# A hybrid attention and state-space layer on one core: the state-space products as tiles of the TensorE array, the result transposes in the input's PSUM bank, one table load per pair, table copies on GpSimd

## The chip, the cores and the metric

The kernel runs on one core of one Trainium2 chip. The metric is device time in microseconds (us) of one execution, taken as the median of several runs. The engines of the core are named as the profile names them: PE is TensorE (PEld its weight loads), DVE is VectorE, ACT is ScalarE, POOL is GpSimd, SP is SyncE, which here issues most DMAs. A "pass" below is one PE record of the profile: a float32 matmul is recorded as two passes, a float32r or bf16 one as one.

## The reference

One decoder layer over 2048 tokens of width 1024, float32:

```python
h = rmsnorm(x, g_mix) * (1 + sc_m) + sh_m          # sc, sh, gt: six vectors, silu(c) @ w_ada + b_ada
q, k, v, f_logit, u = split(h @ w_in)              # 512, 512, 512, 8, 512 columns
attn = rmsnorm(forgetting_attention(q, k, v, log_sigmoid(f_logit + b)), g_attn_out)   # 8 heads x 64
ssm  = rmsnorm(s5_ssm(u, ...), g_ssm_out)
x = x + gt_m * (concat([attn, ssm]) @ w_out)
h = rmsnorm(x, g_ffn) * (1 + sc_f) + sh_f
gate, val = split(h @ w_up)                        # 2 x 2816 columns
x = x + gt_f * ((silu(causal_dwconv(gate)) * val) @ w_down)
return rmsnorm(x, g_final)

def s5_ssm(u, ...):                                # 32 groups x 16 channels, 64 complex states each
    bu = einsum(u, ((lam_bar - 1) / lam) * b)      # lam_bar = exp(lam * dt)
    h  = scan over time: h[t] = lam_bar * h[t-1] + bu[t]
    z  = gelu(real(einsum(h, c)) + d_skip * u)
    return z * sigmoid(z @ w_glu + b_glu)          # per group, 16 x 16
```

## The kernel before

Large products are written as three float32r products of high and low parts. The tokens are worked in four blocks of 512 (`NB`, `TB`). The order in which instructions stand on each engine is not that of the source: a scheduler sets it when the program is built, from priorities (`tc.high_priority()` around `ssm`), from the buffers that the pools have, and from its own times.

The state-space part has two stages.

**Tables** (`ssm_tables`). The 32 groups are 16 pairs; a pair's two groups of 64 states fill the 128 partitions. Four batches `q` of four pairs each build, on DVE, powers of the eigenvalues times the output and input matrices (`f_re`, `f_im`, `e_re`, `e_im`) and rotations (`c_t_`, `s_t_`), and write them to DRAM: `tab_d[q]`, 1024 columns per pair (256 for the input, 256 cosine, 256 sine, 256 for the output from the state), and `tt_d[q]`, one 128x128 Toeplitz matrix per group (8 steps x 16 channels). The Toeplitz entries come from PE products of `bbr`/`bbi` (64 rows, 16 columns) with `f_re`/`f_im` (lines 797 and 798), one group after the other in one PSUM bank (`prep_ps`; `misc_ps = prep_ps` in this function). DVE copies them out (line 799), adds the skip term (lines 802 and 804), and eight DMAs per half write shifted copies from a zero-padded tile `kz` (line 807). The same bank serves the transposes of `e_re`/`e_im` (line 812).

**Pairs** (`ssm`). Time is cut into 256 chunks of 8 steps. For pair `p`, `stage_a` loads the tables and two tiles `ft` whose off-diagonal halves stay zero (lines 833 to 841), transposes the input (`in_ps`, line 853), makes the chunk sums `ss_ps` with the 64-column halves of the array (line 861), and DVE turns, scans and turns back (lines 866 to 879, result `hs`). `stage_b`, written one pair later, makes `y` of each group as one Toeplitz product and two products from the state (lines 887 to 889, 128 rows each), then GELU and GLU on ACT and DVE (lines 892 to 907, product `g_ps` line 901), transposes the result (`tr_ps`, line 912) and copies it to `vout` (line 915), which goes to `ssm_d` (line 941). PSUM holds one bank each: `in` (in_ps, ss_ps), `y` (y_ps), `out` (g_ps, tr_ps).

What stands around the pairs on PE are the projections of q, k (line 485) and v (line 452), and attention of block 0: lines 967 (row maxima), 1012 to 1015 (scores), 1033 and 1037 (times v). After the last pair, `mix_t(0)` loads the `ssm_d` rows, squares them (line 1211), takes a reciprocal root in small DVE steps (lines 185 to 195), scales the rows (line 1217), transposes them (line 1221), and `out_proj(0)` follows (line 1247). The up and down products of the MLP need its result.

Of the kernel before, what the change touches and what calls it, by code (L numbers as in the profile page):

```python
# [12 lines left out]
F32 = mybir.dt.float32  # L13
# [3 lines left out]
AF = mybir.ActivationFunctionType  # L17
ALU = mybir.AluOpType
# [4 lines left out]
P = 128  # L23
# [102 lines left out]
def hybrid_layer(ctx, tc, x, c_t, w_ada, b_col, gains, w_flat, bf_row, a_re, a_im, log_dt,  # L126
# [535 lines left out]
    def ssm_tables(pp):  # L662
        misc_ps = prep_ps
# [12 lines left out]
        Q.dma_start(ci, sc_im)  # L676
        ds_t = tl("ds", [16, NG])
        Q.dma_start(ds_t, dskip)

# [38 lines left out]
        V.tensor_tensor(out=fi, in0=fi, in1=den, op=ALU.mult)  # L718
        bbr, bbi, t16 = tl("bbr", [P, NPAIR, 16]), tl("bbi", [P, NPAIR, 16]), tl("t16", [P, NPAIR, 16])
        b3 = [P, NPAIR, 16]  # L720
# [34 lines left out]
        def batches(marks):  # L755


            kz = tl("kz", [16, 4, 16, 16])
            G.memset(kz[:, :, 0:8, :], 0.0)
            kt = kz[:, :, 8:16, :]  # L760
            for q in range(4):
                with tc.issue_after(marks[q].ins):
# [28 lines left out]

                    for half in range(2):
                        ps = misc_ps()
                        rs = slice(half * 64, half * 64 + 64)
                        for pr in range(4):
                            po = ps[0:16, pr * P : (pr + 1) * P]
                            T.matmul(po, lhsT=bbr[rs, 4 * q + pr, :], rhs=f_re[rs, pr, 0:8, :], start=True, stop=False)
                            T.matmul(po, lhsT=bbi[rs, 4 * q + pr, :], rhs=f_im[rs, pr, 0:8, :], start=False, stop=True)
                        V.tensor_copy(kt, ps[0:16, :].rearrange("c (g m d) -> c g m d", g=4, m=8))
                        dg = tl("dg", [16, 4, 16])  # L800
                        dsq = ds_t.rearrange("c (q p h) -> c q h p", q=4, h=2)[:, q, half, :]
                        V.tensor_tensor(out=dg, in0=ident[0:16, 0:16].unsqueeze(1).broadcast_to([16, 4, 16]),
                                        in1=dsq.unsqueeze(2).broadcast_to([16, 4, 16]), op=ALU.mult)
                        V.tensor_tensor(out=kt[:, :, 0, :], in0=kt[:, :, 0, :], in1=dg, op=ALU.add)
                        dst = tt_d[q].rearrange("(p h) k n -> h k p n", h=2)[half]
                        for j in range(8):
                            Q.dma_start(dst[j * 16 : (j + 1) * 16], kz[:, :, 8 - j : 16 - j, :].rearrange("c g m d -> c g (m d)"))
                    for pr in range(4):
                        wb = tl("wb", [P, 2 * P])
                        ps = misc_ps()  # L810
                        for a, e in enumerate((e_re, e_im)):
                            T.transpose(ps[:, a * P : (a + 1) * P], e[:, pr].rearrange("p j c -> p (j c)"), ident)
                        A.copy(wb, ps[:, 0 : 2 * P])
                        Q.dma_start(td[:, pr, 0:256], wb)
# [7 lines left out]
    def ssm(sp, sps):  # L822
# [3 lines left out]
        V.tensor_scalar(out=hb, in0=hb, scalar1=0.5, scalar2=None, op0=ALU.mult)  # L826
        fts = [sp.tile([P, 2, 2, P], F32, name=f"ft{i}", bufs=1) for i in range(2)]
        for ft in fts:
            G.memset(ft, 0.0)

        def stage_a(p, vin):
            tab = sp.tile([P, 768], F32, name="tab", tag="tab")
            Q.dma_start(tab, tab_d[p // 4][p % 4, :, 0:768])
            ft = fts[p % 2]
            for g in range(2):
                rs = slice(g * 64, g * 64 + 64)
                Q.dma_start(ft[rs, :, g, :], tab_d[p // 4][p % 4, rs, 768:1024].rearrange("p (a n) -> p a n", a=2))
            ttg = sp.tile([P, 2, P], F32, name="ttg", tag="ttg")
# [43 lines left out]
        def stage_b(p, vout, ft, ttg, glt, ug, hs):  # L882

            yp = sps.tile([P, 512], F32, name="y_ps", tag="y", bufs=1)
            for g in range(2):
                yo = yp[:, g * 256 : (g + 1) * 256]
                T.matmul(yo, lhsT=ttg[:, g, :], rhs=ug[:, g, :], start=True, stop=False)
                T.matmul(yo, lhsT=ft[:, 0, g], rhs=hs[:, 0, 0:256], start=False, stop=False)
                T.matmul(yo, lhsT=ft[:, 1, g], rhs=hs[:, 1, 0:256], start=False, stop=True)

            y2 = sp.tile([P, 512], F32, name="y2", tag="y2", bufs=1)
# [3 lines left out]
            z = sp.tile([P, 512], F32, name="z", tag="z")  # L895
# [3 lines left out]
            th = sp.tile([P, 512], F32, name="th", tag="th")  # L899
            for g in range(2):  # L900
                T.matmul(gp[:, g * 256 : (g + 1) * 256], lhsT=glt[:, g, :], rhs=z[:, g * 256 : (g + 1) * 256],
                         start=True, stop=True)
            for g in range(2):
                A.activation(th[:, g * 256 : (g + 1) * 256], gp[:, g * 256 : (g + 1) * 256], AF.Tanh, scale=0.25,
                             bias=hb[:, 2 * p + g : 2 * p + g + 1])
            o4 = th
            V.scalar_tensor_tensor(out=o4, in0=th, scalar=1.0, in1=z, op0=ALU.add, op1=ALU.mult)
            c0 = (p % 4) * 32
            pt = sps.tile([P, 512], F32, name="tr_ps", tag="out", bufs=1)
            for kb in range(2):  # L910
                for g in range(2):
                    T.transpose(pt[:, (2 * kb + g) * P : (2 * kb + g + 1) * P],
                                o4[:, g * 256 + kb * P : g * 256 + (kb + 1) * P], ident)
            for kb in range(2):
                A.activation(vout[kb][:, :, c0 : c0 + 32].rearrange("k t (g c) -> k g t c", g=2),
                             pt[:, kb * 256 : (kb + 1) * 256].rearrange("k (g t c) -> k g t c", g=2, t=8), AF.Copy, scale=0.25)

# [1024 lines left out]
```

## Time and profile before

| | |
|---|---|
| median of 3 runs | 2587.67 us (2587.0 to 2597.44) |
| the profiled execution | 2591.18 us, span 2589.5 us, mean granted TensorE clock 0.983 |
| busy share | PE 96%, PEld 79%, DVE 79%, ACT 48%, POOL 6% |
| table stage, first to last Toeplitz product | 82.6 to 248.8 us |
| pairs, first chunk sum to last result transpose | 350.8 to 577.5 us |
| first product of `out_proj(0)` | 622.3 us |

Times in the profile are counted from the start of the span. The profiled execution took 3.5 us more than the median. Rows of the timeline give the start, the duration (successive equal instructions merged, with their count) and, in brackets, the idle time before and what ended it; passes overlap, so the distance from start to start is what a pass costs, not its duration. Rows of the windows give the length, then busy time and records of PE, PEld, DVE, ACT and POOL, then the granted clock, the DMA engines' busy share and their GB/s.

### The profile page before, as it was taken

How to read it: one execution, taken by the hardware profiler on the slowest of the kernel's cores; microseconds unless marked ns; L12 is line 12 of the kernel's file. 1: busy time of each engine (PE TensorE's matmuls, PEld its weight loads, DVE VectorE, ACT ScalarE, POOL GpSimd, SP SyncE). 2: the span in 40 equal slices, each digit the busy share in tenths (PEclk: the TensorE clock that was granted, in tenths of full speed). 3: DMA queues.
4: the chain of work that ended last, by engine and by line, in shares of the span. 5: the costliest groups of instructions: out<-in, count | busy, mean ns of one | idle time of the engine just before them, and what ended most of it. 6: DMA issues, size and time to landing. Idle time of an engine off the chain costs nothing.

```text
span 2589.5 us, 35781 instructions
## 1 busy us (share of the span) xinstructions
PE 2494.1 (96%) x12107; PEld 2044.2 (79%) x12107; DVE 2048.6 (79%) x3954; ACT 1253.0 (48%) x2122; POOL 151.7 (6%) x160
## 2 busy tenths in 40 slices
PE   6899999998999999999999999999989999999997
PEld 3788877887788888888878888888768888887876
DVE  7989688976787878877877777776589889886777
ACT  3323255654454545555555655556554555553213
POOL 0001000000000000000000000000002333320000
PEclk8999999999899999999999999999999999999998
DMA  8477987667556655656556555556733443447573
GB/s 313 153 256 223 309 257 210 200 184 244 178 185 219 209 185 184 196 179 211 189 198 226 185 179 186 177 184 219 256 101 130 166 160 134 159 153 286 196 279 119
DMA packets 269608, 516.37 MB, mean 199 GB/s; under 512 B 27985, under 2 KB 114897, under 8 KB 269425
## 3 DMA queue, kind: packets, MB, share of 16 engines
q1 hardware_dynamic: 267600, 508.84, 59.6%
q0 software_dynamic: 1280, 4.20, 0.4%
q8 instruction: 96, 1.57, 0.3%
q10 hardware_dynamic: 544, 1.05, 0.1%
q14 instruction: 88, 0.71, 0.1%
HBM read 374.32 MB, written 139.59 MB: 198 GB/s over the span
## 4 chain that ended last, share of the span: by engine, by line
PE 73%; DMA 10%; DVE 10%; ACT 2%; issue 2%; SPq 2%; POOL 0%; POOLq 0%; ACTq 0%; DVEq 0%
PE ff_ps L1273 18%; PE ff_ps L1247 6%; PE up_x L1397 5%; PE up_z L1397 4%; PE up_y L1397 4%; PE ff_ps L1305 3%; PE ff_ps L1307 3%; PE ff_ps L1306 3%; PE o_ps L1033 2%; PE o_ps L1037 2%; DMA wada<-in_w_ada 2%; PE qs_ps L485 2%; PE acc_x L1627 2%; DMA w_raw<-in_w_flat 2%; PE vq_ps L485 1%
## 5 line engine op out<-in xcount | busy, mean ns | idle before, releaser
L86 ACT CAST w_hi<-w_raw 128x1024 fp32r<-128x1024 f32 (+4 forms) x187 | 173.6, 929 | 273.3 <-DMA w_raw<-in_w_flat 63.4
L1273 PE MATMUL ff_ps<-h_hi,w_hi 128*128 128x512 f32 x704 | 276.7, 394 | 1.0 <-ACT h_hi L403 0.8
L1273 PE MATMUL ff_ps<-h_hi,w_lo 128*128 128x512 f32 x704 | 276.7, 393 | 0.9 <-DMA w_lo<-wlo 0.9
L1273 PE MATMUL ff_ps<-h_lo,w_hi 128*128 128x512 f32 x704 | 276.8, 393 | 0.0
L87 DVE TENSOR_TENSOR w_lo<-w_raw,w_hi 128x1024 fp32r<-128x1024 f32 (+4 forms) x187 | 199.6, 1067 | 54.1 <-ACT w_hi L86 48.9
L1024 DVE TENSOR_TENSOR pl<-pf,ph 128x512 fp32r<-128x512 f32 (+1 forms) x320 | 194.5, 617 | 23.3 <-ACT ph L1023 22.6
L1023 ACT CAST ph<-pf 128x512 fp32r<-128x512 f32 (+1 forms) x320 | 178.0, 568 | 58.6 <-PE o_ps L1033 54.8
L1032 DVE TENSOR_TENSOR acc<-acc,pf 128x512 f32<-128x512 f32 (+2 forms) x264 | 159.2, 604 | 45.1 <-ACT pf L1022 39.5
L1273 PEld LDWEIGHTS ff_ps<-h_hi,w_hi 128*128 128x128 f32 x704 | 132.7, 189 | 29.0 <-ACT h_hi L403 1.5
L1273 PEld LDWEIGHTS ff_ps<-h_hi,w_lo 128*128 128x128 f32 x704 | 132.8, 189 | 28.6 <-DMA w_lo<-wlo 1.3
L1022 ACT ACTIVATE pf<-sc_ps 128x512 f32<-128x512 f32 (+3 forms) x184 | 96.6, 528 | 121.0 <-PE sc_ps L1013 74.7
L1273 PEld LDWEIGHTS ff_ps<-h_lo,w_hi 128*128 128x128 f32 x704 | 132.8, 189 | 27.5 <-issue 0.3
L121 ACT CAST w_hi<-w_raw 128x1024 fp32r<-128x1024 f32 (+2 forms) x100 | 96.7, 967 | 106.2 <-PE ff_ps L1273 50.8
L1306 PE MATMUL ff_ps<-act_lo,w_hi 128*128 128x512 f32 x352 | 138.2, 393 | 0.0
L1307 PE MATMUL ff_ps<-act_hi,w_lo 128*128 128x512 f32 x352 | 138.1, 393 | 0.0
L1305 PE MATMUL ff_ps<-act_hi,w_hi 128*128 128x512 f32 x352 | 137.8, 394 | 0.0
L1033 PE MATMUL o_ps<-ph,vv 128*128 128x512 f32 (+1 forms) x320 | 121.2, 379 | 1.7 <-ACT ph L1023 1.5
L1037 PE MATMUL o_ps<-pl,vv 128*128 128x512 f32 (+2 forms) x312 | 116.6, 376 | 2.1 <-DVE pl L1024 1.9
L1397 PE MATMUL up_x<-hh,w_hi 128*128 128x512 f32 x352 | 110.9, 395 | 3.4 <-ACT hh L400 1.9
L1397 PE MATMUL up_z<-hh,w_hi 128*128 128x512 f32 x308 | 96.6, 395 | 3.1 <-ACT w_hi L86 3.1
L86 ACT CAST w_hi<-s 128x1024 fp32r<-128x1024 f32 (+2 forms) x66 | 62.3, 947 | 72.9 <-DVE s L1598 32.4
L1021 POOL MEMSET pf<- 128x128 f32 x32 | 6.6, 206 | 1401.7 <-DVE pl L1024 1171.9
(673 smaller groups left out, 6928.2 us busy)
## 6 DMA issues: line engine op xcount, KB each, us to landing
w_raw<-in_w_flat SPq DMA_DIRECT2D x193, 512.0 KB
w_lo<-wlo SPq DMA_DIRECT2D x68, 512.0 KB
wlo<-w_lo SPq DMA_DIRECT2D x52, 512.0 KB
kb<-kb SPq DMA_DIRECT2D x80, 256.0 KB
vv<-v SPq DMA_DIRECT2D x80, 256.0 KB
w_raw<-in_w_flat SPq DMA_DIRECT2D x40, 384.0 KB
w_raw<-in_w_flat SPq DMA_DIRECT2D x40, 320.0 KB
wada<-in_w_ada SPq DMA_DIRECT2D x48, 256.0 KB
```

What stands on the lines that cost most here:

```text
L86: nc.scalar.copy(hi[:, :n], raw[:, :n])
L87: nc.vector.tensor_tensor(out=lo[:, :n], in0=raw[:, :n], in1=hi[:, :n].bitcast(F32), op=ALU.subtract)
L1023: A.copy(ph[:, cs], pf[:, cs])
L1024: V.tensor_tensor(out=pl[:, cs], in0=pf[:, cs], in1=ph[:, cs].bitcast(F32), op=ALU.subtract)
L1032: eng.tensor_tensor(out=acc[j][:, cs], in0=acc[j][:, cs], in1=pf[:, cs], op=ALU.add)
L1033: T.matmul(o_ps[:, cs], lhsT=vt[:, i, :], rhs=ph[:, cs], start=first, stop=False)
L1037: T.matmul(o_ps[:, cs], lhsT=vt[:, i, :], rhs=pl[:, cs], start=False, stop=(b > 0 and ch == b - 1 and i == 3))
L1273: T.matmul(ps, lhsT=lt, rhs=rt, start=(n == 0), stop=(n == 23))
L1305: T.matmul(ps, lhsT=a, rhs=ah[:, ts], start=(c == 0), stop=False)
L1306: T.matmul(ps, lhsT=a, rhs=al[:, ts], start=False, stop=False)
L1307: mark[0] = T.matmul(ps, lhsT=bb, rhs=ah[:, ts], start=False, stop=(c == n - 1))
L1397: mark[0] = T.matmul(ps, lhsT=lt, rhs=rt, start=(first and n == 0), stop=(n == 11), skip_group_check=not first)
```

## The change

- Toeplitz entries: 16 products of a batch are written as 64-row by 32-column tiles, all `re` terms and then all `im` terms, into eight places of two banks (`prep_ps`, and the bank of `misc_ps`, which also serves the block norms). ACT copies them out, one DVE instruction adds the skip term, GpSimd makes the eight shifted copies of `kz`, and four DMAs per half write them.
- Table load: one DMA of 1024 columns per pair (three buffers) in place of one of 768 and two into `ft`, which is gone.
- `y`: the two Toeplitz products stay; the state products use 64 rows each, group 0 in the upper and group 1 in the lower half of the array, into two PSUM banks. The `y` tile has two banks, and the second halves of them hold the GLU product (`gp`), so that bank `out` is gone; the result transposes go into bank `in`.

```diff
-        ds_t = tl("ds", [16, NG])
-        Q.dma_start(ds_t, dskip)
+        ds_t = tl("ds", [P, 4, 2])
+        V.memset(ds_t, 0.0)
+        for r in range(4):
+            Q.dma_start(ds_t[32 * r : 32 * r + 16], dskip.rearrange("c (q p h) -> p c q h", q=4, h=2)[r])
...
-                    for half in range(2):
-                        ps = misc_ps()
-                        rs = slice(half * 64, half * 64 + 64)
-                        for pr in range(4):
-                            po = ps[0:16, pr * P : (pr + 1) * P]
-                            T.matmul(po, lhsT=bbr[rs, 4 * q + pr, :], rhs=f_re[rs, pr, 0:8, :], start=True, stop=False)
-                            T.matmul(po, lhsT=bbi[rs, 4 * q + pr, :], rhs=f_im[rs, pr, 0:8, :], start=False, stop=True)
-                        V.tensor_copy(kt, ps[0:16, :].rearrange("c (g m d) -> c g m d", g=4, m=8))
...
-                        for j in range(8):
-                            Q.dma_start(dst[j * 16 : (j + 1) * 16], kz[:, :, 8 - j : 16 - j, :].rearrange("c g m d -> c g (m d)"))
+                    pss = [prep_ps()[:, 0:P], misc_ps()[:, 0:P]]
+                    for n, (w, f) in enumerate(zip(bb, (f_re, f_im))):
+                        for pr in range(4):
+                            for half, ps in enumerate(pss):
+                                rs = slice(half * 64, half * 64 + 64)
+                                T.matmul(ps[32 * pr : 32 * pr + 32], lhsT=w[rs, 4 * q + pr : 4 * q + pr + 2, :],
+                                         rhs=f[rs, pr, 0:8, :], start=(n == 0), stop=(n == 1))
+                    for half, ps in enumerate(pss):
+                        kt = tl("kt", [P, P], bufs=2)
+                        A.copy(kt, ps)
+                        V.scalar_tensor_tensor(out=kt[:, 0:16], in0=idr, scalar=ds_t[:, q, half : half + 1], in1=kt[:, 0:16],
+                                               op0=ALU.mult, op1=ALU.add)
+                        for j in range(8):
+                            G.tensor_copy(kz[:, j, j:8, :], kt[:, 0 : (8 - j) * 16].rearrange("c (m d) -> c m d", d=16))
+                        for pr in range(4):
+                            Q.dma_start(tt_d[q][2 * pr + half].rearrange("(j c) n -> c j n", c=16),
+                                        kz[32 * pr : 32 * pr + 16].rearrange("c j m d -> c j (m d)"))
...
-            tab = sp.tile([P, 768], F32, name="tab", tag="tab")
-            Q.dma_start(tab, tab_d[p // 4][p % 4, :, 0:768])
-            ft = fts[p % 2]
-            for g in range(2):
-                rs = slice(g * 64, g * 64 + 64)
-                Q.dma_start(ft[rs, :, g, :], tab_d[p // 4][p % 4, rs, 768:1024].rearrange("p (a n) -> p a n", a=2))
+            tab = sp.tile([P, 1024], F32, name="tab", tag="tab", bufs=3)
+            Q.dma_start(tab, tab_d[p // 4][p % 4])
+            ft = tab[:, 768:1024].rearrange("p (a n) -> p a n", a=2)
...
-            yp = sps.tile([P, 512], F32, name="y_ps", tag="y", bufs=1)
+            both = sps.tile([P, 2, 512], F32, name="y_ps", tag="y", bufs=1)
+            yp, gp = both[:, :, 0:256], both[:, :, 256:512]
             for g in range(2):
-                yo = yp[:, g * 256 : (g + 1) * 256]
-                T.matmul(yo, lhsT=ttg[:, g, :], rhs=ug[:, g, :], start=True, stop=False)
-                T.matmul(yo, lhsT=ft[:, 0, g], rhs=hs[:, 0, 0:256], start=False, stop=False)
-                T.matmul(yo, lhsT=ft[:, 1, g], rhs=hs[:, 1, 0:256], start=False, stop=True)
+                T.matmul(yp[:, g], lhsT=ttg[:, g, :], rhs=ug[:, g, :], start=True, stop=False)
+            for a in range(2):
+                for g in range(2):
+                    rs = slice(g * 64, (g + 1) * 64)
+                    T.matmul(yp[:, g], lhsT=ft[rs, a], rhs=hs[rs, a, 0:256], start=False, stop=(a == 1))
...
-            gp = sps.tile([P, 512], F32, name="g_ps", tag="out", bufs=1)
...
-            pt = sps.tile([P, 512], F32, name="tr_ps", tag="out", bufs=1)
+            pt = sps.tile([P, 2, 256], F32, name="tr_ps", tag="in", bufs=1)
```

The change also moves instructions, since the scheduler sets the order anew. Below are rows of the order on PE and DVE, line numbers of each kernel's own (in the changed kernel 863 is the chunk sum, 889 and 893 the Toeplitz and state products, 904 the GLU product, 913 the result transpose, 855 the input transpose).

PE before, at the chunk sum of the third pair from the end; 452 and 485 are projections, `sc_ps` and `o_ps` attention:

```order
L861 MATMUL ss_ps<-ug,tab 64x256 x4
L485 MATMUL qs_ps<-h_lo,w_hi 128x512
L1012 MATMUL sc_ps<-qb,kb 128x384
L1013 MATMUL sc_ps<-qa_3940,ka_3944 128x384
L1015 LDWEIGHTS identb
L1015 MATMUL sc_ps<-mask_t,identb 128x128
L912 MATMUL tr_ps<-ident,th 128x128 x4
L887 MATMUL y_ps<-ug,ttg 128x256
L1033 MATMUL o_ps<-ph,vv 128x512
L967 MATMUL sc_ps<-ka_3943,qa_3939 128x256
```

PE in the changed kernel, from the chunk sum of the fourth pair from the end (pair 12) to the state products of the same pair:

```order
L863 MATMUL ss_ps<-ug,tab 64x256 x4
L904 MATMUL y_ps<-z,glt 128x256 x2
L967 MATMUL qs_ps<-ka_3982,qa_3977 128x512
L889 MATMUL y_ps<-ug,ttg 128x256 x2
L967 MATMUL vq_ps<-ka_3981,qa_3977 128x512
L913 MATMUL tr_ps<-ident,th 128x128 x4
L855 MATMUL in_ps<-ident,uc 128x128 x4
L967 MATMUL vq_ps<-ka_3982,qa_3977 128x512
L863 MATMUL ss_ps<-ug,tab 64x256 x4
L340 MATMUL sc_ps<-ones,ada_mid 128x1 x4
L967 MATMUL sc_ps<-ka_3981,qa_3977 128x256
L893 MATMUL y_ps<-hs,tab 128x256 x4
```

Before, the q, k and v projections of blocks 2 and 3 stand among the last pairs and behind them; in the changed kernel they are used up ahead of pair 12, and what stands among the last four pairs is attention.

PE before, at the last result transpose (the first transposes of line 1221 come 149 rows later):

```order
L485 MATMUL vq_ps<-h_hi,w_hi 128x512
L912 MATMUL tr_ps<-ident,th 128x128 x4
L980 MATMUL sc_ps<-ident,mneg 4x128
L1012 MATMUL sc_ps<-qb,kb 128x512
L485 MATMUL vq_ps<-h_lo,w_hi 128x512
```

PE in the changed kernel, at the same place (the first transposes of line 1221 come 23 rows after the last result transpose):

```order
L904 MATMUL y_ps<-z,glt 128x256 x2
L913 MATMUL tr_ps<-ident,th 128x128 x4
L967 MATMUL sc_ps<-kx_7288,qa_3977 128x512
L967 MATMUL vq_ps<-kx_7288,qa_3977 128x512
L967 MATMUL sc_ps<-kx_7288,qa_3977 128x512
L967 MATMUL qs_ps<-kx_7288,qa_3977 128x512
L1012 MATMUL sc_ps<-qb,kb 128x512
L1013 MATMUL sc_ps<-qa_3978,ka_7283 128x512
```

The rows between the last transpose of the pairs and `mix_t(0)` went from 149 (mostly projections) to 23 (attention of block 1).

DVE before, within the reciprocal root of `mix_t(0)`:

```order
L195 SCALAR_TENSOR_TENSOR rs_y<-rs_t,rs_i 128x4
L193 TENSOR_TENSOR rs_t<-rs_y 128x4
L194 SCALAR_TENSOR_TENSOR rs_t<-rs_t,rs_v 128x4
L195 SCALAR_TENSOR_TENSOR rs_y<-rs_t,rs_y 128x4
L193 TENSOR_TENSOR rs_t<-rs_y 128x4
```

DVE in the changed kernel, the same steps:

```order
L195 SCALAR_TENSOR_TENSOR rs_y<-rs_t,rs_i 128x4
L1032 TENSOR_TENSOR acc_7881<-acc_7881,pf 128x512
L978 TENSOR_REDUCE mneg<-mx 128x4
L193 TENSOR_TENSOR rs_t<-rs_y 128x4
L1024 TENSOR_TENSOR pl<-pf,ph 128x512
L194 SCALAR_TENSOR_TENSOR rs_t<-rs_t,rs_v 128x4
L1032 TENSOR_TENSOR acc_7881<-acc_7881,pf 128x512
L195 SCALAR_TENSOR_TENSOR rs_y<-rs_t,rs_y 128x4
L1024 TENSOR_TENSOR pl<-pf,ph 128x512
```

Wide attention instructions now stand between the small steps.

More of the change, by code (lines that the diff above doesn't have):

```diff
@@ L755, in batches @@
         def batches(marks):
-            kz = tl("kz", [16, 4, 16, 16])
-            G.memset(kz[:, :, 0:8, :], 0.0)
-            kt = kz[:, :, 8:16, :]
+            kz = tl("kz", [P, 8, 8, 16])
+            for j in range(1, 8):
+                G.memset(kz[:, j, 0:j, :], 0.0)
+            idr = tl("idr", [P, 16])
+            V.reduce_max(out=idr, in_=ident.rearrange("k (r c) -> k c r", r=4)[:, 0:16, :], axis=AX.X)
             for q in range(4):
@@ L808, in batches @@
                     for pr in range(4):
                         wb = tl("wb", [P, 2 * P])
-                        ps = misc_ps()
+                        ps = prep_ps()
                         for a, e in enumerate((e_re, e_im)):
```

33 lines of the change are left out of this document (12 added, 21 removed).

## The prediction

> **What bounds the kernel now.** I read the page first: the span, the busy shares and the chain that ended last.
>
> ```profile
> span 2589.5 us, 35781 instructions
> PE 2494.1 (96%) x12107; PEld 2044.2 (79%) x12107; DVE 2048.6 (79%) x3954; ACT 1253.0 (48%) x2122; POOL 151.7 (6%) x160
> ...
> PE   6899999998999999999999999999989999999997
> ...
> PE 73%; DMA 10%; DVE 10%; ACT 2%; issue 2%; SPq 2%; POOL 0%; POOLq 0%; ACTq 0%; DVEq 0%
> ```
>
> TensorE is busy 96% of the span and nearly full in every slice of 65 us, the table stage (82 to 272 us) included. So a pass that goes away shortens the span by its distance to the next one, and an idle stretch put in front of PE lengthens it by its own length. Only 95 us of idle time are there to lose. The second view is the table of windows, at the places that the change touches: ahead of the pairs, the pairs, from the last result transpose to `mix_t(0)`, and from there to `out_proj(0)`.
>
> ```profile
> core 0: us, PE busy (x) PEld busy (x) DVE busy (x) ACT busy (x) POOL busy (x), PEclk, DMA share, GB/s
> 300.00:360.00 60.00, 54.10 (x334) 46.13 (x334) 32.58 (x70) 22.31 (x42) 0.79 (x3) 0.97 0.92 279
> 351.00:577.00 226.00, 223.92 (x1235) 180.91 (x1232) 195.07 (x406) 124.03 (x258) 1.75 (x7) 0.99 0.70 206
> 577.00:598.00 21.00, 20.80 (x152) 19.27 (x151) 11.08 (x31) 9.88 (x25) 0.20 (x1) 1.00 0.87 265
> 598.00:622.00 24.00, 17.54 (x134) 15.85 (x132) 18.04 (x44) 11.96 (x20) 0.00 (x0) 0.93 0.85 256
> ```
>
> During the pairs PE lacks 2.1 us of 226, but DVE is 86% busy: it is a close second. PE stays full between 577 and 598, while the kernel waits for the result rows to come back; it loses 6.5 us just before `out_proj(0)`.
>
> **Products of y.** Before, one group's three products stand 0.43 us apart, so six per pair take 2.58 us. The nearest row for half-array tiles is the chunk sum, which splits the columns; the changed products split the rows.
>
> ```profile
> 363.15 0.59 PE L889 MATMUL y_ps<-hs,ft 128*128 128x256 f32 x2
> 363.58 0.59 PE L887 MATMUL y_ps<-ug,ttg 128*128 128x256 f32 x2
> 364.01 0.59 PE L888 MATMUL y_ps<-hs,ft 128*128 128x256 f32 x2
> ...
> 350.24 0.39 PE L485 MATMUL vq_ps<-h_lo,w_hi 128*128 128x512 f32 x1
> 350.46 0.39 PE L485 MATMUL vq_ps<-h_hi,w_lo 128*128 128x512 f32 x1
> 350.78 1.08 PE L861 MATMUL ss_ps<-ug,tab 128*64 128x256 f32 x8
> 351.79 0.48 PE L887 MATMUL y_ps<-ug,ttg 128*128 128x256 f32 x1
> ```
>
> Four chunk sums (eight passes) take 1.01 us, where one after the other they would take 4 x 0.43 = 1.72. The projection ahead of them would have been followed after 0.22 or 0.23 us; the chunk sum starts 0.32 us behind it, so entering costs 0.09 us, and I take as much for leaving. After the change a pair has two Toeplitz products (0.86) and four state products, two at a time (0.86), and two switches (0.18): 1.90 us. Saved: 0.68 x 16 = **-10.9 us**. Bounds: -13.8 without a price of switching; +2.9 if row halves do not overlap at all (six products as before, and the switches).
>
> The Trainium skill, "TensorEngine Tiling (Array Packing)", section "Tiling Modes", says that changing the tiling mode drains the array. The 0.09 us ahead of the chunk sum agrees that a switch has a price, but is less than the 0.16 us by which a pass outlasts its spacing (0.38 against 0.22); at 0.16 per switch this term would be -8.6 us.
>
> **Toeplitz entries.** Before, eight products of half a batch, and eight halves:
>
> ```profile
> 95.44 0.39 PE L797 MATMUL prep_ps<-tb_f_re,tb_bbr 64*16 64x128 f32 x2
> 95.67 0.38 PE L798 MATMUL prep_ps<-tb_f_im,tb_bbi 64*16 64x128 f32 x2
> ...
> 97.29 0.39 PE L452 MATMUL proj_ps<-wu_hi,h_hi 128*128 128x264 f32 x1
> ```
>
> One half takes 1.85 us, all of them 14.8. Eight tiles at once would leave 2 x 0.23 and a switch, 0.62 per batch (-12.3 us); two at a time 1.94 per batch (-7); none side by side 0. I take **-10**, nearer to the first, since these tiles differ in rows and in columns, and columns are seen to overlap above.
>
> **Copies, loads and DMA issues.** The rows that go, and the nearest ones for what comes:
>
> ```profile
> L799 DVE COPY tb_kz<-prep_ps x8: 669/672/678, 93.7 to 250.5; 16x512 f32<-16x512 f32 x8
> L813 ACT COPY tb_wb<-prep_ps x16: 352/373/378, 104.6 to 271.4; 128x256 f32<-128x256 f32 x16
> L829 POOL MEMSET ft<- x2: 528/530/531, 299.6 to 300.1; 128x512 f32 x2
> L807 SPq DMA_DIRECT2D tt<-tb_kz x64: 302/425/1467, 96.1 to 256.3; - x64
> L833 SPq DMA_DIRECT2D tab<-tab x16: 319/410/1473, 303.5 to 523.4; - x16
> L837 SPq DMA_DIRECT2D ft<-tab x32: 585/618/1163, 305.1 to 533.3; - x32
> ```
>
> DVE loses eight copies of 0.67 us and the small multiplications; ACT gains eight of at most 0.37 (half as wide as line 813). GpSimd gains 64 copies on its idle queue, at most 64 x 0.53 = 34 us by its 128x512 memset, and a quarter of that by width; a batch has 40 us. SP issues 32 fewer `tt` DMAs (0.43 us each) and 32 fewer `ft` loads (0.62 each), and three more for the skip vector. All of it lies beside PE work: the last table is built at 271.4, the first load of one leaves at 303.5 us. I cost it **0**. Gain at best: the idle time of PE from 300 to 360, 5.9 us. Loss at worst, where no cover is left: one half's eight GpSimd copies (8 x 0.53) twice plus four issues on the way to the last batch's tables (2 x (4.2 + 1.7) = 12), so +12.
>
> **The pairs' end.** Here the order matters more than the products. In the changed order the projections are used up by pair 12, and from its chunk sum to the last result transpose PE holds 29 rows of 512 columns (0.23 each, 6.7 us), 18 f32 products of 256 (0.43, 7.7), 32 half-array rows two at a time (6.9) and some 65 narrower ones (about 0.13, 8.5): about 30 us. On DVE the same stretch, from the first turn of pair 12 to the last gate product of pair 15, holds 120 rows. Their prices:
>
> ```profile
> 431.09 0.69 DVE L866 TENSOR_TENSOR m<-ss_ps,tab 128x512 f32<-128x512 f32 x1 [1.09 <-PE ss_ps L861]
> 431.70 0.68 DVE L867 TENSOR_TENSOR m<-ss_ps,tab 128x512 f32<-128x512 f32 x1
> ...
> 432.41 0.42 DVE L868 TENSOR_TENSOR m<-m,m 128x256 f32<-128x256 f32 x1
> 432.76 0.42 DVE L869 TENSOR_TENSOR m<-m,m 128x256 f32<-128x256 f32 x1
> 433.09 1.27 DVE L872 TENSOR_TENSOR_SCAN gg<-r,m 128x256 f32<-128x256 f32 x2
> 434.39 0.69 DVE L875 TENSOR_TENSOR hs<-gg,tab 128x512 f32<-128x512 f32 x1
> ...
> L971 DVE CUSTOM_DVE_ANT_0 sc_ps<-sc_ps,mask_q 128x256 f32<-128x256 f32 x6 | 2.5, 424 | 0.6 <-PE sc_ps L967 0.6
> ```
>
> 55 of 512 columns at 0.61 are 33.6 us, 25 of 256 at 0.35 are 8.8, eight scans at 0.65 are 5.2, eleven masked maxima at 0.42 are 4.6, and 21 others about 4: 56 us. So PE can not be done before DVE, and waits about 57 - 30 = **+27 us** in this stretch, if DVE never waits either. What makes it wait: the next chunk sum needs bank `in`, and the result transposes of the pair before now stand in that bank, so the sums of pair p follow the gate product and the copies of pair p-2. Both ends: 12, if DVE rows of attention that I put in the stretch are late in their own inputs and fall behind it; 36, if the chain through PE, ACT and DVE of one pair after the other adds to DVE's work.
>
> **From the last transpose to out_proj.** Before:
>
> ```profile
> 577.18 0.38 PE L912 MATMUL tr_ps<-ident,th 128*128 128x128 f32 x2
> 588.70 0.63 ACT L1211 ACTIVATE sq<-row 128x512 f32<-128x512 f32 x1 [1.36 <-DMA row<-ssm]
> 598.05 0.49 DVE L1217 TENSOR_SCALAR row<-row,rs_y 128x512 f32<-128x512 f32 x1
> 598.70 0.49 PE L1221 MATMUL ff_ps<-ident,row 128*128 128x128 f32 x3
> ...
> 619.96 0.80 PE L967 MATMUL qs_ps<-ka,qa 66*128 66x512 f32 x1 [5.14 <-DVE mx L971]
> 622.29 0.78 PE L1247 MATMUL ff_ps<-yt,w_hi 128*128 128x512 f32 x1
> ```
>
> The rows go to DRAM and back (11.5 us to the first square), the reciprocal root runs on DVE, and 21.5 us after the last result transpose the transposes of line 1221 start. The 149 PE rows in between cover it now (20.80 of 21 us busy). In the changed order 23 rows stand there, 23 x 0.23 = 5.3 us, so 16 us stay open; the wide DVE rows that now stand within the root lengthen it by up to 5, and the clock is lower after an idle stretch (0.93 in the last window). I take **+18**, between 12 (the round trip a third shorter, DMA being less busy by then) and 24. The transposes wait at the head of PE's queue, so attention and the MLP behind them wait too. What was idle ahead of `out_proj(0)` before (6.5 us, of which 5.14 at 619.96) I take as gone, since attention had its time by then: **-6**, between -6.5 and 0.
>
> **Sum.** -10.9 - 10 + 0 + 27 + 18 - 6 = +18 us. The profiled execution took 2591.2, so 2609; it stood 3.5 us above the median of 2587.7, so the forecast is 2606 us.
>
> **Rivals.**
> - *Faster: the new waits do not appear.* Where DVE's attention rows in the last pairs stand behind late inputs, and the chunk sums are ready earlier than I chain them, PE stays full as between 351 and 577, where it lost 2.1 us. Then the 20.9 us of saved passes come straight back: 2587.7 - 21 = 2567. It decides for faster once the stalls at both places stay under 8 us. For it: 14% of DVE's time was free. Against it: 23 rows can not cover 21 us.
> - *No measurable change: the waits are half as long.* 12 + 15 at the two places, against 21 saved and 6 no longer lost, give about 0 to +9: near 2592.
> - *Row halves do not overlap.* Then y costs +3 instead of -11 and the entries gain nothing: 2606 + 24 = 2630. Against it: the column halves overlap. No row of before shows rows split. The Trainium skill, same page, says that different tiles work independently, which speaks against this rival too.
>
> **How the numbers follow.** 0.5% (12.9 us) is about what a measurement here can tell from no change. Chances: 0.45 for the sum (2600 to 2622 by its own), 0.12 for row halves without overlap (about 2630), 0.25 for waits half as long (2580 to 2600), 0.18 for faster (2560 to 2574). So slower 0.57, the same 0.25, faster 0.18. The range 2570 to 2632 takes in all but most of the faster case and the far ends of the waits.
>
> **What would show it.** In the changed profile: state products starting in pairs, four within 0.9 to 1.1 us; the 16 entry products within 0.6 to 2 us; DVE over 95% busy over the last three pairs with PE idle by 20 us or more, released by DVE or ACT; line 1221 released by DVE's scaled rows after 12 us or more of idle; nothing waiting on `tab` or `ttg` at the first pair. Wrong it would be if PE were over 95% busy in the last pairs, if state products stood 0.43 apart, or if pairs waited for tables.

## The result, and the profile after

The changed kernel takes 2665.9 us (median of 6 runs) against 2596.2 us of the kernel before in the same runs: 1.0281 times as long, 95% interval 1.0257 to 1.0305. The profiled execution has a span of 2668.5 us, 79 us more than before. Slower was forecast, but at 2606 us with an upper end of 2632.

The head of the page:

```profile
span 2668.5 us, 35799 instructions
...
PE 2514.3 (94%) x12107; PEld 2044.0 (77%) x12107; DVE 2047.3 (77%) x3942; ACT 1258.6 (47%) x2130; POOL 185.4 (7%) x228
...
PE   6887989998699999999999999999989999999997
```

PE ran as many passes as before, idles 154 us where it idled 95, and is "busy" 20 us longer although some of its passes now run side by side: part of its work ran at a lower granted clock, as the windows below show.

The windows below have the same six places as ends in both kernels, in order: the first Toeplitz entry, the first chunk sum, the chunk sum of pair 12, the end of the last result transpose, the first transpose of line 1221, the first product of `out_proj(0)`. Columns are those of the prediction: length, busy time of the engines, granted clock, DMA share, GB/s. The kernel before:

```profile
82.60:350.80 268.20, 250.43 (x1629) 222.63 (x1628) 220.73 (x524) 85.19 (x166) 17.16 (x26) 0.97 0.78 248
350.80:501.00 150.20, 148.18 (x847) 119.83 (x846) 133.70 (x284) 82.08 (x175) 0.82 (x4) 0.99 0.71 213
501.00:577.80 76.80, 76.74 (x398) 61.94 (x398) 62.32 (x124) 42.20 (x84) 0.93 (x3) 1.00 0.67 193
577.80:598.70 20.90, 20.70 (x151) 19.29 (x151) 10.94 (x33) 9.75 (x25) 0.20 (x1) 1.00 0.90 271
598.70:622.30 23.60, 17.14 (x130) 15.29 (x128) 17.68 (x42) 11.86 (x20) 0.00 (x0) 0.92 0.84 257
```

The changed kernel:

```profile
84.20:374.90 290.70, 248.51 (x1630) 218.52 (x1630) 217.58 (x507) 87.39 (x173) 50.69 (x88) 0.94 0.73 230
374.90:617.50 242.60, 232.80 (x1367) 189.46 (x1366) 186.67 (x387) 123.14 (x247) 1.45 (x7) 0.97 0.69 212
617.50:687.80 70.30, 52.98 (x217) 33.41 (x217) 57.10 (x128) 28.78 (x64) 2.49 (x6) 0.78 0.38 121
687.80:714.60 26.80, 10.55 (x24) 6.50 (x24) 10.13 (x37) 8.37 (x19) 0.00 (x0) 0.52 0.54 153
714.60:720.60 6.00, 4.34 (x27) 3.87 (x28) 5.64 (x17) 4.34 (x8) 0.00 (x0) 0.78 0.15 44
```

I count as lost what PE idles, and its busy time times the part of the clock that was not granted (rounded to 0.01, so rough over long stretches).

| stage | before: idle + clock | after: idle + clock | more lost | forecast |
|---|---|---|---|---|
| tables to first chunk sum | 17.8 + 7.5 | 42.2 + 14.9 | 32 | 0 |
| first chunk sum to that of pair 12 | 2.0 + 1.5 | 9.8 + 7.0 | 13 | 0 |
| pair 12 to last transpose | 0.1 + 0 | 17.3 + 11.7 | 29 | 27 |
| to line 1221 | 0.2 + 0 | 16.3 + 5.1 | 21 | 18 |
| to out_proj(0) | 6.5 + 1.4 | 1.7 + 1.0 | -5 | -6 |

Together 90 us. Passes that run side by side take back some 19. The products themselves, on the timeline of the changed kernel:

```profile
385.59 0.40 PE L485 MATMUL vq_ps<-h_hi,w_hi 128*128 128x512 f32 x1
385.92 1.13 PE L893 MATMUL y_ps<-hs,tab 64*128 64x256 f32 x8
386.99 0.50 PE L1013 MATMUL sc_ps<-qa,ka 67*128 67x512 f32 x1
...
203.98 0.39 PE L485 MATMUL qs_ps<-h_hi,w_lo 128*128 128x512 f32 x1
204.30 0.42 PE L804 MATMUL prep_ps<-tb_f_re,tb_bbr 64*32 64x128 f32 x8
204.54 0.40 PE L804 MATMUL prep_ps<-tb_f_im,tb_bbi 64*32 64x128 f32 x8
204.87 0.50 PE L485 MATMUL vq_ps<-h_hi,w_hi 128*128 128x512 f32 x1
```

Four state products (eight passes) take 1.07 us: row halves run two at a time, as column halves did. They also start 0.10 us late (0.33 us behind the pass ahead of them, where 0.23 is usual). With the two Toeplitz products (0.86) that is 2.03 us per pair in place of 2.58, so 8.8 us over 16 pairs. Eight entry products take 0.57 us in place of 1.85, so about 10.2 us over eight halves, if all are like this one. Of the 79 us, 90 - 19 = 71 are placed; 8 are not, which is within the rounding of the clock (0.005 of the 1900 us of PE work behind `out_proj(0)` alone is some 10).

The idle time between the last result transpose and line 1221 (16.3 us) is nearly all one wait, and not the one forecast:

```profile
687.06 0.66 PE L913 MATMUL tr_ps<-ident,th 128*128 128x128 f32 x4 [1.66 <-DVE th L908]
702.85 0.77 PE L967 MATMUL sc_ps<-kx,qa 66*128 66x512 f32 x1 [15.14 <-DMA kx<-kb]
...
714.56 2.20 PE L1221 MATMUL ff_ps<-ident,row 128*128 128x128 f32 x12 [0.20 <-DVE row L1217]
```

The attention of block 1 that should have covered the gap waited 15.1 us for its own load of `kx`, which SP issued only at 696.87, behind the stores of the last pairs and the row loads of `mix_t(0)`. It ran after the idle time, and line 1221 waited 0.20 us.

### The profile page after: what moved, and what is told of

Same layout as the page of the kernel before. It is cut to its first block, busy times and chain, and to the rows that moved or that the text cites. A ratio compares the mean times of both kernels' runs of the same rounds, so it can differ in the third digit from the quotient of the medians.

```text
span 2668.5 us, 35799 instructions
## 1 busy us (share of the span) xinstructions
PE 2514.3 (94%) x12107; PEld 2044.0 (77%) x12107; DVE 2047.3 (77%) x3942; ACT 1258.6 (47%) x2130; POOL 185.4 (7%) x228
## 4 chain that ended last, share of the span: by engine, by line
PE 76%; DVE 10%; DMA 7%; issue 2%; SPq 2%; ACT 2%; POOL 1%; POOLq 0%; ACTq 0%; DVEq 0%
PE ff_ps L1273 18%; PE ff_ps L1247 7%; PE up_x L1397 6%; PE up_z L1397 4%; PE up_y L1397 4%; PE ff_ps L1305 3%; PE ff_ps L1306 3%; PE ff_ps L1307 3%; PE o_ps L1033 2%; PE o_ps L1037 2%; PE qs_ps L485 2%; DMA wada<-in_w_ada 2%; PE acc_x L1627 2%; PE proj_ps L452 2%; PE vq_ps L485 2%
## 5 line engine op out<-in xcount | busy, mean ns | idle before, releaser
L452 PE MATMUL proj_ps<-wu_hi,h_hi 128*128 128x264 f32 (+1 forms) x256 | 78.7, 314 | 24.8 <-ACT h_hi L403 19.4
```

## Experiments: which part loses

Four kernels, each against the kernel before on the same chip (2590.1 us there).

**The pairs part alone**: `ssm` of the changed kernel, `ssm_tables` of the kernel before.

> The changed pairs with the tables built as before. Theory: of the 70 us lost, about 20 are lost in the table stage and 50 in the pairs and behind them, and the two add up; so this kernel takes 2640 to 2656 us, its table stage is as long as before, and PE idles about 35 us between the chunk sum of pair 12 and line 1221. Rival: the pairs are late because their tables are; then it is within 15 us of the kernel before (2581 to 2611).

**The tables part alone**: `ssm_tables` changed, `ssm` as before.

> The changed tables with the pairs as before. Theory: the table stage alone loses 15 to 30 us (2611 to 2626), with about 38 us of PE idle between 82 and 300 us as in the changed kernel, and 20 us of full PE between the last result transpose and line 1221. Rival (late tables cause the pairs' loss): about 2660.

**One edit to the kernel before:**

```diff
-            pt = sps.tile([P, 512], F32, name="tr_ps", tag="out", bufs=1)
+            pt = sps.tile([P, 512], F32, name="tr_ps", tag="in", bufs=1)
```

> The kernel before with one edit: the result transposes go into bank in. Theory: it is this sharing that lets the scheduler run out of projections before the last pairs, so the tail and the gap to line 1221 open without any other part: 2635 to 2665. Rival: the loss comes from y and the GLU product sharing a tile, or from the array tiles; then within 12 us of before (2584 to 2608).

**One edit to the changed kernel:** the Toeplitz DMAs leave SP's queue.

```diff
-                            Q.dma_start(tt_d[q][2 * pr + half].rearrange(...
+                            G.dma_start(tt_d[q][2 * pr + half].rearrange(...
```

> The changed kernel, but the 32 DMAs that write the Toeplitz matrices are issued by GpSimd behind its own copies, and not by SP. Theory: in the table stage SP stands 18 us behind those copies, and the stores and loads queued behind them hold ACT and then PE; so 12 to 25 us come back (2641 to 2654) and PE's waits for line 403 and 821 shrink to half or less. Rival: the loss comes from the transposes of e_re and e_im with their one copy buffer, or from GpSimd slowing DVE; then within 6 us of the changed kernel (2660 to 2672).

Measured: the pairs part 2649.8 us, 1.0230 (1.0215 to 1.0245); the tables part 2614.9 us, 1.0098 (1.0081 to 1.0115); the bank alone 2655.2 us, 1.0247 (1.0229 to 1.0264); the Toeplitz DMAs by GpSimd 2657.1 us, 1.0255 (1.0239 to 1.0272).

The two parts lose separately, about 60 and 25 us, somewhat more than the whole change (73). The bank by itself is enough for the loss of the pairs: moving the result transposes into bank `in`, with full-array products and the old tables, costs 65 us. Less the 9 us that it does not save, 56 of the 60 us of the pairs part are there, the same within the intervals. The last edit took SP's wait for GpSimd (18.3 us in the table stage) out of the profile, but its interval overlaps that of the changed kernel, and the first chunk sum came only 2 us earlier (372.9 us). So SP's queue is not the main cause in the table stage, against my theory.

## Experiments: what a shared bank does to the pairs

**The cover held back.** My prediction said that the projections are used up too early. In the changed kernel those of block 3 are held:

```diff
+        hold = tc.issue_after(pair_mark[10].ins) if b in (3,) else ExitStack()
+        with hold:
+            proj_qkv(b, h, qs_ps, each=mid)
-        proj_qkv(b, h, qs_ps, each=mid)
```

> The changed kernel with one edit: the projections of block 3 may not be placed ahead of pair 10's chunk sum, so that 94 rows stand between the last result transpose and line 1221, where 24 stood, and 313 from the chunk sum of pair 12 to that transpose, where 111 stood. Theory: the pairs lose because their cover is used up; 40 to 55 us come back (2611 to 2626). Rival: the chain of one pair through bank in is itself the limit, whatever stands beside it: less than 15 us back (2651 to 2670).

**The same with the repairs of the tables** that the next section describes (two buffers for `wb`, Toeplitz DMAs by GpSimd):

> The changed kernel with the projections held to pair 10, two buffers for wb and the Toeplitz DMAs from GpSimd. Theory: all losses but some 8 us at line 1221 (55 rows stand there) are gone and the 21 us of saved passes show: 2570 to 2592. Rival: the repairs do not add up, since the projections held back are missing in the middle of the pairs: 2600 to 2630.

Measured: 2658.6 us, 1.0263 (1.0239 to 1.0286), and 2648.6 us, 1.0224 (1.0202 to 1.0245). The cover stood where I wanted it, and almost nothing came back: the interval of the hold overlaps that of the changed kernel (1.0257 to 1.0305). With the repairs of the tables about 15 us came back, far from the 2570 to 2592 us expected. Windows of the first one, two ahead of the hold's end and one from the last result transpose to the transposes of `mix_t(0)`:

```profile
460.00:500.00 40.00, 36.78 (x259) 30.95 (x258) 36.71 (x79) 25.24 (x54) 0.21 (x1) 0.95 0.81 257
500.00:540.00 40.00, 29.47 (x138) 18.93 (x137) 36.56 (x88) 21.71 (x46) 0.41 (x2) 0.80 0.53 162
661.70:698.70 37.00, 27.50 (x85) 18.84 (x85) 27.84 (x79) 21.13 (x46) 0.94 (x3) 0.71 0.62 175
```

PE now idles 10.5 us between 500 and 540 at a clock of 0.80, and the gap at the end, 94 rows long in the order, still has 9.5 idle. The stage from first chunk sum to last transpose lasts some 290 us (313 in the changed kernel) in place of 227, and what PE has to do in it does not fill that, wherever it is put.

**The pairs by themselves.** So I looked at a pair's own pace: the projections of blocks 2 and 3 and the attention of block 0 are held behind the last chunk sum, for three bank layouts. Each of these three ran once.

```diff
+    with tc.issue_after(pair_mark[15].ins):
+        attention((0,))
-    attention((0,))
```

> The kernel before with the projections of blocks 2 and 3 and the attention of block 0 held behind the last pair's chunk sum, so that the pairs run with almost nothing beside them: the chain of a pair by itself. Not meant to be fast. Theory: the 16 chunk sums stand 8 to 10.5 us apart, under the 12.6 us of the full kernel.

> The same, with the result transposes in bank in. Theory: the shared bank makes the chain of a pair longer, by 2.5 us or more: chunk sums 11 to 14 us apart. Rival: the chain is the same within 0.5 us a pair, and only the order in which the scheduler places the other work loses the time.

> The changed pairs with the result transposes in the y banks, old tables, and the projections of blocks 2 and 3 and attention of block 0 held behind the last pair's chunk sum, to see a pair's own pace. Not meant to be fast. Theory: y of the next pair waits for the result's copies, and the pace is 10.5 to 13 us a pair, against 7.44 with three banks and 12.0 with the transposes in bank in. Rival: about 7.5, and the time goes elsewhere.

The timeline of PE, chunk sums only, with the three banks of the kernel before:

```profile
424.06 1.08 PE L863 MATMUL ss_ps<-ug,tab 128*64 128x256 f32 x8
431.50 1.08 PE L863 MATMUL ss_ps<-ug,tab 128*64 128x256 f32 x8
438.94 1.08 PE L863 MATMUL ss_ps<-ug,tab 128*64 128x256 f32 x8
```

With the result transposes in bank `in`:

```profile
399.22 1.08 PE L863 MATMUL ss_ps<-ug,tab 128*64 128x256 f32 x8
405.08 1.97 PE L863 MATMUL ss_ps<-ug,tab 128*64 128x256 f32 x8 [0.81 <-ACT ug L858]
423.79 1.08 PE L863 MATMUL ss_ps<-ug,tab 128*64 128x256 f32 x8
```

With them in the `y` banks (changed pairs):

```profile
432.15 1.08 PE L857 MATMUL ss_ps<-ug,tab 128*64 128x256 f32 x8
445.81 1.08 PE L857 MATMUL ss_ps<-ug,tab 128*64 128x256 f32 x8
```

The pace is 7.44 us with three banks; with the shared bank pairs come in twos, 24.6 us for two here, so 12 us a pair (375.4 to 522.0 us for twelve pairs: 12.2); with the `y` banks 13.66. The windows of the first two kernels, over twelve pairs each, say what sets the pace:

```profile
371.98:461.26 89.28, 70.72 (x385) 51.33 (x384) 83.75 (x168) 47.48 (x107) 0.00 (x0) 1.00 0.53 154
375.43:522.00 146.57, 97.71 (x386) 65.72 (x385) 87.08 (x168) 45.84 (x108) 0.00 (x0) 0.81 0.36 101
```

With three banks DVE is 94% busy: its work sets 7.44 us. With the shared bank DVE does the same 168 instructions at 59%, and the waits of PE between 380 and 520 us name the chain (engine, line, what it waited for, us in total, times, longest):

```profile
PE g_ps L903 <- DVE z L898: 26.3, 11, 4.5
PE in_ps L855 <- ACT vout L917: 9.3, 12, 0.8
PE tr_ps L914 <- DVE m L869: 6.5, 5, 1.3
PE ss_ps L863 <- ACT ug L858: 4.6, 6, 0.8
```

The input transposes of a pair wait until the result of an earlier pair is copied out of the bank (line 917), and the GLU product waits for GELU with nothing beside it. The end of one pair and the beginning of another no longer run side by side.

The bank is not busy all that time. It serves in turn the input transposes, the chunk sums and the result transposes:

```profile
407.71 0.68 DVE L869 TENSOR_TENSOR m<-ss_ps,tab 128x512 f32<-128x512 f32 x1
...
419.77 0.60 PE L914 MATMUL tr_ps<-ident,th 128*128 128x128 f32 x4
...
421.17 0.66 PE L855 MATMUL in_ps<-ident,uc 128*128 128x128 f32 x4 [0.80 <-ACT vout L917]
```

From the end of the last read of the sums (408.39) to the next result transposes (419.77) nothing uses it, 11.4 of the 24.6 us, while y, GELU and GLU of that result are made; the input transposes of the next pair stand behind it. So the pace of 12 us is that of sharing in the order that the scheduler set. No run tries another order of the three in one bank.

In the full kernel before, a pair had 12.6 us (350.8 to 540.4 over fifteen), of which it needed 7.44 by itself; the rest was room for waits behind other work. At 12 us alone there is none, and with other work on DVE, ACT and PE between the steps the pairs of the changed kernel take 19 us each (374.9 to 660.3 over fifteen).

**The transposes in the y banks**, in the full kernel with the old tables:

```diff
-            pt = sps.tile([P, 2, 256], F32, name="tr_ps", tag="in", bufs=1)
+            pt = yp
```

> The changed pairs with the old tables (2650 us), with the result transposes in the halves of the y banks that y no longer needs, so that bank in is free after the chunk sums. Theory: any sharing that lets a pair's end hold the next pair's start costs pace, here y of the next pair waits for the copies of the result; a part comes back: 2615 to 2640. Rival A: only bank in costs: 2575 to 2600. Rival B: nothing back: 2645 to 2660.

Measured 2647.4 us, 1.0214 (1.0190 to 1.0238), the same as the pairs part within its interval. Rival B: nothing back, as the pace of 13.66 us fits. So it is not bank `in` in particular: the loss is as large where the transposes share the `y` banks. In both, the result transposes, which stood in bank `out`, share a bank with an earlier stage.

## Experiments: what the tables lose

All of these have the pairs as before, and are to be read against the tables part (1.0098). Edits, each on top of the changed `ssm_tables`:

```diff
# two buffers for wb
-                        wb = tl("wb", [P, 2 * P])
+                        wb = tl("wb", [P, 2 * P], bufs=2)
# rotation writes by SP
-                        G.dma_start(td[:, r0 : r0 + 2, 256:512], ...
+                        Q.dma_start(td[:, r0 : r0 + 2, 256:512], ...
# copies on ACT
-                            G.tensor_copy(kz[:, j, j:8, :], ...
+                            A.copy(kz[:, j, j:8, :], ...
# a bank of the projections
-                    pss = [prep_ps()[:, 0:P], misc_ps()[:, 0:P]]
+                    pss = [prep_ps()[:, 0:P], in_ps.tile([P, 512], F32, name="tz_ps", tag="proj", bufs=4)[:, 0:P]]
```

Two buffers for `wb`:

> The changed tables with the pairs as before (2615 us), and a second buffer for wb, the tile through which ACT copies the transposes of e_re and e_im out. Theory: in the new order the four transposes of a batch stand close together, each copy waits for the write of the one before, and PE stands 11 us behind them; so 6 to 11 us come back (2604 to 2609). Rival: SP's wait for GpSimd is what delays those writes, and a buffer more changes little: 2611 to 2618.

Two buffers, and the Toeplitz DMAs by GpSimd:

> As the last, and the Toeplitz DMAs issued by GpSimd. Theory: with both the buffer and SP's queue free the whole loss of the table stage goes, and the 10 us of saved passes show: 2582 to 2598. Rival: DVE and GpSimd slow each other, or the new order holds PE elsewhere: 2604 or more.

Those two, and the rotation writes by SP:

> The changed tables with the pairs as before, two buffers for wb, the Toeplitz DMAs from GpSimd, and now the rotation writes (tab from rc and rs), which GpSimd issued, from SP. Theory: GpSimd's copies also hold the rotation writes in its own queue, DVE waits for the buffer (5.9 us in one place) and PE for DVE; so the rest of the loss goes: 2585 to 2602. Rival: the order or the shared misc bank holds PE: 2605 to 2615, as without this edit (2610).

Two buffers and the copies on ACT:

> The changed tables with the pairs as before, two buffers for wb, and the 64 shifted copies on ACT and not on GpSimd; all DMAs from the queues of the changed kernel. Theory: what hurts is that two DMA queues stand behind slow GpSimd copies; 64 copies of about 0.25 us on ACT cost 16 us of an engine that is 48% busy: 2585 to 2604. Rival: the loss does not come from GpSimd: 2606 to 2616; or ACT's copies hold h_hi as much: the same.

Two buffers, and seven of eight copies left out (`if j == 0`, with `kz` cleared once):

> The changed tables with two buffers for wb and the pairs as before (2611 us), with seven of the eight shifted copies of each half left out (the Toeplitz matrices then lack their shifted diagonals). Theory: the copies and the queues behind them are 10 to 20 us of the loss: 2590 to 2600. Rival: the rest of the loss is the order and the banks: 2604 to 2612.

Two buffers, copies on ACT, a bank of the projections:

> The kernel with the copies on ACT and two buffers for wb (2605 us), with the second bank of the Toeplitz tiles taken from the four of the projections and not from misc, which the block norms use. Theory: the norm chain (misc, lines 365 and 371) waits behind the Toeplitz copy and the projections wait for the norm; 5 to 15 us come back (2588 to 2600). Rival: the bank does not matter: 2601 to 2609.

The bank of the projections alone:

> The changed tables with the pairs as before (2615 us) and one edit: the second bank of the Toeplitz tiles from the projections' four, not from misc. Copies on GpSimd and one wb as in the changed kernel. Theory: the bank is most of the loss: 2593 to 2602. Rival: it helps only where wb and the copies are repaired too: 2606 to 2616.

That bank and two buffers:

> The last, with two buffers for wb; copies on GpSimd. Theory: bank and buffer are all of the loss, GpSimd's copies cost nothing (leaving seven of eight out changed nothing): 2582 to 2594, perhaps under the kernel before by part of the 10 us of saved passes. Rival: copies on ACT were needed: 2596 to 2606.

| kernel | us | against before |
|---|---|---|
| tables part | 2614.9 | 1.0098 (1.0081 to 1.0115) |
| two wb | 2611.0 | 1.0075 (1.0054 to 1.0096) |
| two wb, one copy of eight | 2611.1 | 1.0071 (1.0052 to 1.0089) |
| two wb, Toeplitz DMAs by GpSimd | 2610.3 | 1.0075 (1.0055 to 1.0095) |
| the same, rotation writes by SP | 2601.5 | 1.0051 (1.0031 to 1.0070) |
| two wb, copies on ACT | 2605.0 | 1.0058 (1.0039 to 1.0077) |
| projections' bank | 2604.3 | 1.0056 (1.0041 to 1.0071) |
| projections' bank, two wb | 2603.4 | 1.0051 (1.0037 to 1.0065) |
| projections' bank, two wb, copies on ACT | 2591.2 | 1.0001 (0.9990 to 1.0012) |

The bank alone brings about 11 us; with it and two buffers for `wb`, the copies on ACT in place of GpSimd bring 12 (2603.4 to 2591.2, intervals apart). With the bank still shared, the buffer and the seven copies left out bring little; taking the copies to ACT, or the rotation writes away from behind them in GpSimd's queue, ends 10 to 13 us under the tables part, but their intervals overlap that of the buffer alone. Only the three together bring 24 us; that kernel equals the one before, so what its entries save, some 10 us, is still lost in it. With the bank shared, leaving seven copies out and moving all to ACT can not be told apart by their intervals. Why the copies weigh 12 us once the bank is free, and nothing clear of the intervals while it is shared, is not explained. Windows from 82 to 350 us: before, the tables part, the bank alone, and the last of the table:

```profile
82.00:350.00 268.00, 250.23 (x1630) 222.69 (x1629) 221.28 (x525) 84.75 (x165) 17.16 (x26) 0.97 0.78 248
82.00:350.00 268.00, 227.87 (x1465) 201.17 (x1465) 203.00 (x479) 74.11 (x147) 51.32 (x89) 0.92 0.73 230
82.00:350.00 268.00, 239.05 (x1557) 213.82 (x1558) 206.07 (x484) 77.69 (x154) 47.02 (x89) 0.93 0.76 241
82.00:350.00 268.00, 242.68 (x1620) 215.45 (x1621) 212.76 (x498) 93.12 (x229) 16.21 (x25) 0.96 0.78 249
```

PE had run 165 passes fewer by 350 us with the tables part, and 10 fewer with all three repairs. Where the loss comes up is seen at the last batch of the changed kernel, in rows of PE and then of ACT:

```profile
248.38 0.47 PE L820 MATMUL prep_ps<-ident,tb_e_re 128*128 128x128 f32 x1 [2.00 <-ACT tb_wb L821]
252.48 0.47 PE L820 MATMUL prep_ps<-ident,tb_e_re 128*128 128x128 f32 x1 [3.41 <-ACT tb_wb L821]
260.60 0.59 PE L452 MATMUL proj_ps<-wu_hi,h_hi 128*128 128x264 f32 x1 [6.58 <-ACT h_hi L403]
...
252.06 0.37 ACT L821 COPY tb_wb<-prep_ps 128x256 f32<-128x256 f32 x1 [3.73 <-DMA tab<-tb_wb]
259.56 0.37 ACT L821 COPY tb_wb<-prep_ps 128x256 f32<-128x256 f32 x1 [4.91 <-DMA tab<-tb_wb]
259.83 1.33 ACT L403 ACTIVATE h_hi<-h_f,mod_sm 128x512 fp32r<-128x512 f32 x2
```

ACT waits for the write of `wb`, the next block's `h_hi` stands behind it in ACT's queue, and PE stands behind `h_hi`. That row made me try the buffer first; 4 us came back, within the intervals. What stays open is how much of the bank's 11 us is the norm chain waiting in `misc` and how much the order that the scheduler makes of another bank: each edit sets the order anew, and no run here holds it fixed.

## Why the prediction was right in direction and wrong in size

- **Products.** Right in kind: 8.8 us for y (forecast 10.9) and about 10.2 for the entries (10). Entering costs 0.10 us ahead of the state products (385.59 + 0.23 to 385.92), against 0.09 taken. The rest of the switch, within the group and behind it, is 0.21 (1.07 - 0.86) where I took 0.09 again, though my own row of the chunk sum had 0.15 there (1.01 - 0.86).
- **The pairs' end.** Right in place, and in size partly by luck: 29 us (27). DVE's work there was priced well (57.1 us against a sum of 56, which my next line took as 57), but it was not the limit: DVE was busy 81% of the stretch (80% over the last three pairs, where I had over 95%), since it waits too, and the stretch took 70 us and not 57. PE idles 17 us where I had 27. The other 12 are its clock, 0.78 in this window, for which I had no term. The cause that I gave, cover used up too early, was half of it: the hold showed that the stage is too long for its cover, and with almost nothing beside the pairs the shared bank takes their pace from 7.44 to 12 us. For the same reason the 0 for the pairs up to pair 12 was wrong: they lost 13.
- **The gap to line 1221.** The size was right, 21 us (18), by another wait than the one forecast. I had line 1221 waiting 12 us or more for DVE's rows behind 5 us of attention. It waited 0.20 us, and the attention ahead of it stood 15.1 us for `kx`. That sign of mine failed.
- **Copies, loads and DMA issues, costed at 0 with a bound of +12.** This is the step that failed: the tables part, with 10 us of saved passes in it, costs 25 us, so some 35 us were lost. The copies took 35.7 us, more than the bound of 34 that I had for them and four times the quarter of it that I expected by width, and I called GpSimd's queue idle. A second tenant in the norms' bank was in the diff and had no term at all. My bound came from one batch's path to the tables, but PE did not wait for tables: the first load of one came at 330.0 us, 70 us after the last copy of `wb` (259.6). PE waited for the copies of `wb` themselves and for the projections' inputs, behind the table work in ACT's and DVE's queues. Its two largest waits from 84.2 to 374.9 us were 2.4 us (line 812) and 3.4 in the kernel before:

```profile
PE prep_ps L820 <- ACT tb_wb L821: 12.2, 6, 3.4
PE proj_ps L452 <- ACT h_hi L403: 10.4, 6, 6.6
```

- **The sum.** It came to +18 where some +70 were measured. Of the 52 between, 32 are the table stage, 13 the pairs up to pair 12, and the rest the small misses above.
- **Rivals.** That row halves do not overlap was false. The waits appeared, and in full.

No version beat the kernel before; the best, with the Toeplitz tiles and the pairs as before, equals it.

## What to carry to other kernels

Before a PSUM bank is given to a second stage, measure the pace of the loop by itself with and without it: here 9 us of saved passes were paid with some 5 us in each pair's own pace, and holding other work back for the pairs did not buy that back. A step costed at nothing needs every tenant of its bank and its queue named. A total that comes out right can hide a wrong wait: read which wait ended the idle time. Idle time of PE cost more than its length here: the granted clock was 0.78 in the window with 25% idle and 0.52 in that with 61%, against 0.99 and 1.00 in the windows of the kernel before with under 2%.

## What the runs showed of the hardware

The same 64 copies took a median of 505 ns on GpSimd in the changed kernel and 247 ns on ACT, and on GpSimd eight of them took 7.21 us at one place and 1.56 us at another. DVE was busy for all of the first stretch (142.35 to 149.56) and for none of the second (220.17 to 221.73); at 236.18 eight took 2.09 us with DVE busy for 0.72 of them. So the copies were slow where DVE worked beside them; no run changes this alone, so what of DVE's work holds them is not shown. The first two rows are the groups by line in the changed kernel and in the last of the table above, then two of the timeline:

```profile
L812 POOL COPY tb_kz<-tb_kt x64: 193/505/2048, 94.4 to 250.3; 128x128 f32<-128x128 f32 x8, 128x112 f32<-128x112 f32 x8, 128x96 f32<-128x96 f32 x8, 128x80 f32<-128x80 f32 x8
L812 ACT COPY tb_kz<-tb_kt x64: 198/247/302, 92.8 to 243.2; 128x128 f32<-128x128 f32 x8, 128x112 f32<-128x112 f32 x8, 128x96 f32<-128x96 f32 x8, 128x80 f32<-128x80 f32 x8
...
142.35 7.21 POOL L812 COPY tb_kz<-tb_kt 128x128 f32<-128x128 f32 x8 [13.76 <-DVE tb_kt L809]
220.17 1.56 POOL L812 COPY tb_kz<-tb_kt 128x128 f32<-128x128 f32 x8 [3.88 <-DMA tt<-tb_kz]
```

Products on half of the array's rows overlap as well as those on half of its columns (1.07 us against 1.01 us for eight passes). The Trainium skill, "TensorEngine Tiling (Array Packing)", section "Tiling Modes", has a change of mode drain the array; the 0.10 us ahead of the products here is less than the 0.16 us by which a pass outlasts its spacing, and 0.21 us more come within the group and behind it.
